# First tokens loaded in 4 KB rows, conditioning sums undivided and behind the 1/rms chain, tokens scaled block by block

## The chip, the cores and the metric

The kernel runs on one core of a Trainium2 chip. The metric is the device time of one execution in microseconds (us). TensorE (PE) multiplies matrices and transposes, VectorE (DVE) and ScalarE (ACT) work elementwise, GpSimd (POOL) does slower elementwise work, and SyncE (SP) issues the transfers from and to memory (DMA).

## The reference

A two-layer encoder over 1024 tokens of width 1024. Each layer normalises the tokens, scales and shifts them by a conditioning vector, mixes tokens and adds the result back under a gate:

```python
c_act = jax.nn.silu(c)
for layer in range(DEPTH):
    mod = c_act @ ada_w[layer] + ada_b[layer]
    shift, scale, gate = jnp.split(mod, 3, axis=-1)
    h = rms_norm(x, norm_w[layer]) * (1.0 + scale[:, None, :]) + shift[:, None, :]
    y = even_mixer(h, ...) if layer % 2 == 0 else odd_mixer(h, ...)
    x = x + gate[:, None, :] * y
return rms_norm(x, final_norm)
```

In layer 0 the mixer begins with `proj = h @ w_in`. Everything that the change touches at the start serves to make `h` for the first 512 tokens and to multiply it with the first columns of `w_in`.

## The kernel before

The tokens are held transposed: the model's width lies on the partitions, in eight blocks of 128 (`kc` 0 to 7), and 512 tokens (a half) lie in a row. `xT[half]` is four tiles of 128 x 1024, each with two blocks side by side; `chunk(t, kc)` is one block of 128 x 512. fp32 precision is kept by splitting each factor of a product into a high part (`h`, rounded by a cast) and a low part (`l`, the remainder), so that a product takes three matmuls (`mm3`: high x high, low x high, high x low).

The start goes as follows. The first half's tokens are loaded block by block (`xT_half(0)`), ACT squares each block (`sq`), DVE adds the squares up, and PE transposes the sums so that DVE can reduce them over the width (`ss`). POOL raises the result to the power -1/2 (`r`), PE spreads it over all partitions in PSUM (`rp0`, the 1/rms of each token), and DVE scales the eight blocks by it. This is the 1/rms chain, `rstd_rows`.

Meanwhile the conditioning values are made: for each block `kc` a scale and a shift per channel, each a sum over 1024 products of a loaded row of `ada_t` with `cb` (`ada_sum`, `ada_mods`; results in `mods`). One such sum is a DVE instruction that multiplies, adds up and leaves its total to a short read-out instruction. In the trace it is CUSTOM_DVE_ANT_0 with DVE_READ_ACCUMULATOR2_ANT; in the built order both are called ISA. Before the change a sum is taken in two pieces of 512, into a small tile `ada..`, and one addition makes `mods` of the pieces.

Then, block by block, ACT makes the high part of `h` from the scaled tokens (`hT00h`, with `mods` as scale and bias) and `h` itself (`xT`), DVE subtracts them to the low part (`hT00l`), and PE multiplies four token tiles with two groups of weight columns, 416 wide (`c1_part`, weights `w1.`) and 512 wide (`c3_part`, weights `w3.`): 24 matmuls for a block. The weights are split by ACT (high) and DVE (low), two blocks to a load (`wload`). Behind the eighth block come PE's transposes for the second half's squares and the columns of `w2`.

All instructions are recorded (`Recorder`) and a planner with assumed durations lays them out in time. They are then emitted in the order of its start times, each engine running its own queue in order:

```python
for o in sorted(self.ops, key=lambda o: (o.start, o.i)):
    fn, a, kw = o.call
    fn(*[real(v) for v in a], **{k: real(v) for k, v in kw.items()})
```

That is why nearly every row of the trace bears the line L483. An operation's `after` (set by `behind`) keeps the planner from placing it before another one's planned start. It adds no wait on the chip.

Of the kernel before, what the change touches and what calls it, by code (L numbers as in the profile page):

```python
# [14 lines left out]
ALU = mybir.AluOpType  # L15
# [8 lines left out]
KC = D // P  # L24
# [481 lines left out]
def encoder_kernel(ctx: ExitStack, tc: tile.TileContext, xt, ada_t, w_c1, w_c2, w_c3, w_g0, w_uq, w_ukv, w_out0, w_v1,  # L506
                   w_f1, w_out1, cols_d, rows_d, tabs_d, out, dump=None):
    if dump is None:
# [12 lines left out]
    mhalf = const.tile([P, 16], F32, name="mhalf")  # L521
    tc.nc.vector.memset(mhalf, -0.5)

    nc = rec = Recorder(tc.nc, tc, psum, {"u": U_BUFS, "ua": UA_BUFS, "sm": SM_BUFS}, window=WINDOW,
                        reserve=RESERVE)
# [11 lines left out]
    def SM(name):  # L537
        return rec.tile(smp, [P, 16], F32, name, "sm")
# [13 lines left out]
    def behind(ins, mark):  # L552
        ins.after = mark
        return ins
# [8 lines left out]
    def load(o, i, mark=None):  # L563
        return behind(nc.sync.dma_start(out=o, in_=i), mark)
# [24 lines left out]
    def transposes(outs, ins, last):  # L589
# [3 lines left out]
        for j in order:  # L593
            with issue_after(m_):
                t_ = nc.tensor.transpose(out=outs(j), in_=ins[j], identity=ident)
            if last is not None:
# [5 lines left out]
    mods = const.tile([P, 32], F32, name="mods")  # L602
# [5 lines left out]
                                   op0=ALU.add, op1=ALU.mult)  # L608
    cb = U("cb")
    for j in range(2):  # L610
        pt = PT(f"cb{j}")
        for k in range(4):
# [7 lines left out]
                                   op0=ALU.add, op1=ALU.mult)  # L620
    g0 = const.tile([P, 16], F32, name="g0")
    nc.gpsimd.tensor_scalar(g0, cols[:, C_BG:C_BG + 16], 0.5, 0.0, op0=ALU.mult, op1=ALU.add)
    gcol = const.tile([P, 16], F32, name="gcol")
# [10 lines left out]

    def ada_sum(o, src, scale, first, name, mark, parts):

        s = U(name)
        load(s, src, mark)  # L640
        n = 1024 // parts
        for q in range(parts):
            c = slice(q * n, (q + 1) * n)
            nc.vector.tensor_tensor_reduce(out=s[:, c], in0=s[:, c], in1=cb[:, c], scale=scale,
                                           scalar=0.0 if q else first, op0=ALU.mult, op1=ALU.add, accum_out=o[q])

    def ada_mods(l, kc, mark=None):

        t = SM(f"ada{l}{kc}")
        k = 8 * l + kc  # L650
        for j in range(2):
            o = [t[:, 2 * q + j:2 * q + j + 1] for q in range(2)]
            scale, first = (0.5, cols[:, C_BSH + k:C_BSH + k + 1]) if j else (nwh[:, k:k + 1], a0[:, k:k + 1])
            ada_sum(o, ada_t[l * 24 + 8 * (1 - j) + kc], scale, first, f"ada{l}{kc}{j}", mark, 2)
        nc.vector.tensor_tensor(out=mods[:, 2 * k:2 * k + 2], in0=t[:, 0:2], in1=t[:, 2:4], op=ALU.add)

    def ada_gate(l, b, mark=None):
        for t in range(4 * b, 4 * b + 4):
            k = 8 * l + t
            ada_sum([gcol[:, k:k + 1]], ada_t[l * 24 + 16 + t], 0.25, g0[:, k:k + 1], f"adag{l}{t}", mark, 1)  # L660

    def A_col(l, kc):
        return mods[:, 16 * l + 2 * kc:16 * l + 2 * kc + 1]
# [14 lines left out]
    def rstd_rows(accs, name):  # L678

        n = accs[0].shape[1]  # L680
        nt = n // P
        v = None
        for k, acc in enumerate(accs):
            pt = PA(f"st{name}")
            for j in range(nt):
                m_ = nc.tensor.transpose(out=pt[:, j * P:(j + 1) * P], in_=acc[:, j * P:(j + 1) * P], identity=ident)
            ss = SM("ss")
            nc.vector.tensor_reduce(out=ss[:, 0:nt], in_=pt[:, 0:n].rearrange("p (t c) -> p t c", t=nt), axis=AX.X,
                                    op=ALU.add)
            if k == 0:  # L690
                nc.vector.tensor_scalar(ss[:, 4:4 + nt], ss[:, 0:nt], 1.0 / D, EPS, op0=ALU.mult, op1=ALU.add)
            else:
                nc.vector.scalar_tensor_tensor(out=ss[:, 4:4 + nt], in0=ss[:, 0:nt], scalar=1.0 / D, in1=v, op0=ALU.mult,
                                               op1=ALU.add)
            v = ss[:, 4:4 + nt]
        if name == "x0" and WARM[1]:
            warm(WARM[1], m_)
        r = SM("r")
        nc.gpsimd.tensor_tensor(out=r[:, 0:nt], in0=v, in1=mhalf[:, 0:nt], op=ALU.pow)
        pr = PA(f"rb{name}")  # L700
        for j in range(nt):
            m_ = nc.tensor.transpose(out=pr[:, j * P:(j + 1) * P], in_=r[:, j:j + 1].broadcast_to([P, P]), identity=ident)
        if name == "x0" and WARM[2]:
            warm(WARM[2], m_)
        return pr[:, 0:n]

    def rows_copy(pr, name):
        rb = U(f"rb{name}")[:, 0:pr.proto().shape[1]]
        nc.scalar.copy(rb, pr)
        return rb  # L710
# [51 lines left out]


    xT = {}

    def chunk(t, kc):
        return t[kc // 2][:, (kc % 2) * 512:(kc % 2 + 1) * 512]

    def xT_half(half):
        xT[half] = [U(f"xT{half}{k2}") for k2 in range(4)]  # L770
        acc = U(f"sq{half}")
        if half == 0:
            for kc in range(KC):
                load(chunk(xT[0], kc), xt[0, kc // 2][:, (kc % 2) * 512:(kc % 2 + 1) * 512])
            a, b = acc[:, 0:512], acc[:, 512:1024]
            for kc in range(KC - 1):
                add_squares((a, b)[kc % 2], chunk(xT[0], kc), kc < 2, f"sq0{kc}", nc.vector)
            nc.vector.tensor_tensor(out=a, in0=a, in1=b, op=ALU.add)
            last = U("sq07")[:, 0:512]
            add_squares(last, chunk(xT[0], KC - 1), True, "", None)  # L780
            return rstd_rows([a, last], "x0")
        else:
            eng = nc.vector if SQ_ENG[0] == "dve" else nc.gpsimd
            for k2 in range(4):
                load(xT[half][k2], xt[half, k2])
                add_squares(acc, xT[half][k2], k2 == 0, f"sq{half}{k2}", eng)
            eng.tensor_tensor(out=acc[:, 0:512], in0=acc[:, 0:512], in1=acc[:, 512:1024], op=ALU.add)
        return rstd_rows([acc[:, 0:512]], f"x{half}")
# [3 lines left out]

    marks = {}
    VA = [U(f"VA{j}", F32R).rearrange("p (t g s d) -> p t g s d", t=4, g=2, s=2) for j in range(2)]
    karaw = U("karaw").rearrange("p (t c) -> p t c", t=8)
    ckvraw = U("ckvraw").rearrange("p (t c) -> p t c", t=8)
# [47 lines left out]
    E1, E3 = E_START  # L846
    rp0 = xT_half(0)
    for kc in range(KC):
        c = chunk(xT[0], kc)
        nc.vector.tensor_tensor(out=c, in0=c, in1=rp0, op=ALU.mult)  # L850
    for kc in range(KC):
        ada_mods(0, kc)
        if kc % 2 == 0:
            w1 += wload([w_c1[kc // 2]], 416, f"w1{kc // 2}", hi_eng=START_ENG[0], lo_eng=START_ENG[1])
            w3 += wload([w_c3[kc // 2]], 512, f"w3{kc // 2}", hi_eng=START_ENG[2], lo_eng=START_ENG[3])
        modulate(0, kc, chunk(xT[0], kc), None, hT0[0][kc], "normed")
        for i in range(E1):
            c1_part(i, w1[kc:], [kc])
        for i in range(E3):
            m_ = c3_part(i, w3[kc:], [kc])  # L860
# [5 lines left out]
    rb0 = rows_copy(xT_half(1), "x1")  # L866
# [45 lines left out]
    for g in range(2):  # L912
# [5 lines left out]
        r = rstd_of(ss[:, 0:8], HD, 8)  # L918
# [3 lines left out]
        for b in range(2):  # L922
            for s in range(2):
                nc.vector.tensor_tensor(out=t2[:, :, b * 32 + s * 16:b * 32 + s * 16 + 16],
                                        in0=kr_[:, :, b * 32 + (1 - s) * 16:b * 32 + (1 - s) * 16 + 16],
# [903 lines left out]
```

## Time and profile before

| | |
|---|---|
| median of 3 runs | 1215.26 us (1213.6 to 1216.71) |
| profiled execution, own time | 1213.96 us |
| its span in the trace | 1211.9 us |
| PE busy | 1170.2 us (97% of the span) |
| DVE busy | 933.9 us (77%) |
| ACT busy | 660.4 us (54%) |
| POOL busy | 560.3 us (46%) |

The span is the time from the first to the last instruction in the trace; the 2.06 us between it and the execution's own time lie around it. Busy time is an average over stages with different limits: where an engine is nearly always busy over the whole span, the stretches in which it isn't are to be looked for.

### The profile page before, as it was taken

What the parts mean: (1) busy time and instruction counts of PE and PEld (TensorE: products, weight loads), DVE (VectorE), ACT (ScalarE), POOL (GpSimd) and SP (SyncE); (2) the same over time, 40 slices, a digit from 0 to 9 for tenths busy, and PEclk for the clock granted to TensorE, in tenths of its full rate; (3) what the DMA queues carried; (4) which work ended last, traced back from release to release, by engine and by line L of the source; (5) the groups of instructions that cost most, each with busy time, mean ns of one, the idle gap of its engine ahead of it and who ended that gap; (6) DMA issues with size and microseconds to landing.
All of it is one profiled execution on the core that took longest, in us unless ns stands there. A gap on an engine that the chain in (4) does not pass through costs nothing.

```text
span 1211.9 us, 17927 instructions
## 1 busy us (share of the span) xinstructions
PE 1170.2 (97%) x6320; PEld 987.2 (81%) x6320; DVE 933.9 (77%) x1787; ACT 660.4 (54%) x1348; POOL 560.3 (46%) x551
## 2 busy tenths in 40 slices
PE   6999899999999999999999999899999999999996
PEld 5898778787878778778778888788888888888896
DVE  7976497888687988888789996839876598788343
ACT  4643356666555777787768122227765456653212
POOL 0057764435465555444448233504465265367321
PEclk9999899999999999999999999899999999999999
DMA  9601123131122220101034663100111121045112
GB/s 352 253 1 58 56 83 122 35 105 34 61 68 79 79 70 19 36 1 52 2 143 167 240 250 143 67 18 1 36 53 53 52 88 53 19 166 199 70 71 70
DMA packets 37338, 106.72 MB, mean 88 GB/s; under 512 B 3840, under 2 KB 9472, under 8 KB 37248
## 3 DMA queue, kind: packets, MB, share of 16 engines
q1 hardware_dynamic: 36480, 103.48, 23.7%
q0 software_dynamic: 768, 2.10, 0.7%
q8 instruction: 49, 0.80, 0.3%
q14 instruction: 41, 0.34, 0.1%
HBM read 82.36 MB, written 23.20 MB: 87 GB/s over the span
## 4 chain that ended last, share of the span: by engine, by line
PE 83%; DVE 10%; ACT 3%; issue 1%; DMA 1%; POOL 0%; SPq 0%; POOLq 0%; DVEq 0%; ACTq 0%
PE psum L483 83%; DVE nm L483 2%; DVE hla L483 1%; DVE p L483 1%; DVE hT11l L483 1%; DVE xr L483 1%; ACT q L483 1%; DVE Qa L483 1%; DMA xT<-in_xt 1%; ACT Pa L483 0%; DVE q L483 0%; ACT p L483 0%; DVE hl L483 0%; DVE hlb L483 0%; DVE ada L483 0%
## 5 line engine op out<-in xcount | busy, mean ns | idle before, releaser
L483 DVE TENSOR_REDUCE nm<-psum 128x1 f32<-128x1024 f32 x128 | 155.3, 1217 | 18.9 <-PE psum L483 17.2
L483 POOL TENSOR_SCALAR p<-p,dn 128x384 f32<-128x384 f32 (+1 forms) x128 | 74.1, 596 | 159.1 <-DVE dn L483 79.2
L483 DVE TENSOR_TENSOR hla<-psum,hla 128x512 fp32r<-128x512 f32 x128 | 84.9, 681 | 25.0 <-ACT hla L483 24.5
L483 PE MATMUL psum<-hla,VA 128*128 128x512 f32 x256 | 94.4, 421 | 5.4 <-DVE hla L483 4.0
L483 ACT CAST hla<-psum 128x512 fp32r<-128x512 f32 x128 | 72.5, 593 | 43.5 <-PE psum L483 37.2
L483 PE MATMUL psum<-ident,Pa 128*128 128x128 f32 x512 | 93.8, 272 | 0.8 <-DVE q L483 0.8
L483 POOL TENSOR_SCALAR Pb<-Pb,rs 128x1024 f32<-128x1024 f32 x64 | 71.8, 1124 | 45.6 <-DVE rs L483 43.9
L483 PE MATMUL psum<-hlb,VB 128*128 128x512 f32 x256 | 90.8, 427 | 2.2 <-DVE hlb L483 1.5
L483 POOL TENSOR_SCALAR Pa<-Pa,rs 128x1024 f32<-128x1024 f32 x64 | 76.4, 1198 | 34.8 <-DVE rs L483 32.1
L483 ACT ACTIVATE Pa<-psum,nm 128x1024 f32<-128x1024 f32 x64 | 71.6, 1120 | 32.0 <-DVE nm L483 24.7
L483 DVE TENSOR_TENSOR hlb<-psum,hlb 128x512 fp32r<-128x512 f32 x128 | 82.2, 683 | 7.7 <-ACT hlb L483 6.9
L483 ACT ACTIVATE Pb<-psum,nm 128x1024 f32<-128x1024 f32 x64 | 71.8, 1123 | 25.1 <-DVE nm L483 22.2
L483 PE MATMUL psum<-k,q 128*128 128x512 f32 x256 | 84.0, 399 | 0.2 <-ACT Pb L483 0.2
L483 PE MATMUL psum<-ident,Pb 128*128 128x128 f32 x512 | 79.4, 272 | 0.0
L483 DVE CUSTOM_DVE_ANT_0 p<-psum,bias,rows_g 128x384 f32<-128x384 f32 (+1 forms) x128 | 70.2, 577 | 10.7 <-PE psum L483 9.7
L483 ACT ACTIVATE p<-p,nm 128x384 f32<-128x384 f32 (+1 forms) x128 | 74.0, 585 | 7.1 <-DVE nm L483 7.1
L483 PEld LDWEIGHTS psum<-ident,Pa 128*128 128x128 f32 x512 | 65.0, 140 | 12.5 <-DVE q L483 1.0
L483 ACT CAST hlb<-psum 128x512 fp32r<-128x512 f32 x128 | 68.9, 603 | 9.1 <-PE psum L483 7.8
L483 ACT COPY ot<-psum 64x512 f32<-64x512 f32 x64 | 37.4, 584 | 65.7 <-PE psum L483 65.0
L483 PEld LDWEIGHTS psum<-ident,Pb 128*128 128x128 f32 x512 | 63.2, 140 | 11.2
L483 POOL TENSOR_TENSOR sq<-sq,sq 128x256 f32<-128x256 f32 (+2 forms) x22 | 26.9, 1222 | 79.9 <-ACT sq L483 79.7
L483 PE MATMUL psum<-oTl,wo1h 128*128 128x256 f32 (+1 forms) x192 | 61.1, 319 | 0.0
(749 smaller groups left out, 3672.3 us busy)
## 6 DMA issues: line engine op xcount, KB each, us to landing
ada<-in_ada_t SPq DMA_DIRECT2D x32, 512.0 KB, 8.2
adag<-in_ada_t SPq DMA_DIRECT2D x16, 512.0 KB, 4.8
o<-spill SPq DMA_DIRECT2D x12, 512.0 KB, 6.5
wo0s<-in_w_out SPq DMA_DIRECT2D x8, 512.0 KB, 8.4
xr<-in_xt SPq DMA_DIRECT2D x8, 512.0 KB, 9.6
x_sp<-xr SPq DMA_DIRECT2D x8, 512.0 KB, 3.0
wo1s<-in_w_out SPq DMA_DIRECT2D x8, 512.0 KB, 5.8
x1r<-x_sp SPq DMA_DIRECT2D x8, 512.0 KB, 5.3
```

Of the source, the lines that this page charges most:

```text
L483: fn(*[real(v) for v in a], **{k: real(v) for k, v in kw.items()})
```

## The change

The first half's tokens are loaded as four transfers of 128 rows of 4 KB instead of eight of 128 rows of 2 KB. Each conditioning sum is one instruction over 1024 products that writes straight into `mods`. For layer 0 these sums may not be planned before the POOL power of the 1/rms chain (`late=marks["rstd", "x0"]`). The eight scalings of the tokens no longer stand together: each stands in its block's turn, and only the first reads 1/rms from PSUM. For the other seven ACT copies it into SBUF (`rb0`). The sums of layer 1 are undivided too; the gates' sums (`ada_gate`) were so already.

```diff
-    def ada_sum(o, src, scale, first, name, mark, parts):
+    def ada_sum(o, src, scale, first, name, mark, late=None):
 
         s = U(name)
         load(s, src, mark)
-        n = 1024 // parts
-        for q in range(parts):
-            c = slice(q * n, (q + 1) * n)
-            nc.vector.tensor_tensor_reduce(out=s[:, c], in0=s[:, c], in1=cb[:, c], scale=scale,
-                                           scalar=0.0 if q else first, op0=ALU.mult, op1=ALU.add, accum_out=o[q])
-
-    def ada_mods(l, kc, mark=None):
-
-        t = SM(f"ada{l}{kc}")
+        behind(nc.vector.tensor_tensor_reduce(out=s, in0=s, in1=cb, scale=scale, scalar=first, op0=ALU.mult,
+                                              op1=ALU.add, accum_out=o), late)
+
+    def ada_mods(l, kc, mark=None, late=None):
+
         k = 8 * l + kc
         for j in range(2):
-            o = [t[:, 2 * q + j:2 * q + j + 1] for q in range(2)]
             scale, first = (0.5, cols[:, C_BSH + k:C_BSH + k + 1]) if j else (nwh[:, k:k + 1], a0[:, k:k + 1])
-            ada_sum(o, ada_t[l * 24 + 8 * (1 - j) + kc], scale, first, f"ada{l}{kc}{j}", mark, 2)
-        nc.vector.tensor_tensor(out=mods[:, 2 * k:2 * k + 2], in0=t[:, 0:2], in1=t[:, 2:4], op=ALU.add)
+            ada_sum(mods[:, 2 * k + j:2 * k + j + 1], ada_t[l * 24 + 8 * (1 - j) + kc], scale, first, f"ada{l}{kc}{j}",
+                    mark, late)
...
-        nc.gpsimd.tensor_tensor(out=r[:, 0:nt], in0=v, in1=mhalf[:, 0:nt], op=ALU.pow)
+        marks["rstd", name] = nc.gpsimd.tensor_tensor(out=r[:, 0:nt], in0=v, in1=mhalf[:, 0:nt], op=ALU.pow)
...
-            for kc in range(KC):
-                load(chunk(xT[0], kc), xt[0, kc // 2][:, (kc % 2) * 512:(kc % 2 + 1) * 512])
+            for k2 in range(4):
+                load(xT[0][k2], xt[0, k2])
...
     rp0 = xT_half(0)
     for kc in range(KC):
+        ada_mods(0, kc, late=marks["rstd", "x0"])
         c = chunk(xT[0], kc)
-        nc.vector.tensor_tensor(out=c, in0=c, in1=rp0, op=ALU.mult)
-    for kc in range(KC):
-        ada_mods(0, kc)
+        nc.vector.tensor_tensor(out=c, in0=c, in1=rb0 if kc else rp0, op=ALU.mult)
+        if kc == 0:
+            rb0 = rows_copy(rp0, "x0")
```

How the planner's order moves is seen on two engines. First DVE, before the change, from the end of the first block's sums on (`xT00` holds blocks 0 and 1, `w10l0` and `w30l0` are the weights' low parts of blocks 0 and 1, `ada010` and `ada011` the rows for block 1's scale and shift):

```order
L483 TENSOR_TENSOR mods_81<-ada00_129 128x2
L483 TENSOR_TENSOR w10l0_134<-w10s0_132,w10h0_133 128x832
L483 TENSOR_TENSOR xT00_115<-xT00_115,psum_72 128x512 x2
L483 TENSOR_TENSOR xT01_116<-xT01_116,psum_72 128x512 x2
L483 TENSOR_TENSOR xT02_117<-xT02_117,psum_72 128x512 x2
L483 TENSOR_TENSOR xT03_118<-xT03_118,psum_72 128x512 x2
L483 TENSOR_TENSOR w30l0_137<-w30s0_135,w30h0_136 128x1024
L483 TENSOR_TENSOR hT00l0_92<-xT00_115,hT00h0_88 128x512
L483 ISA ada010_139,ada01_138<-ada010_139,cb_83,a0_85,nwh_84 128x512
L483 ISA ada01_138 128x1
```

The same place on DVE in the changed kernel, from the last step ahead of POOL's power (`ss_127`) on:

```order
L483 SCALAR_TENSOR_TENSOR ss_127<-ss_127,ss_126 128x4
L483 ISA ada000_129,mods_81<-ada000_129,cb_83,a0_85,nwh_84 128x1024
...
L483 ISA ada001_130,mods_81<-ada001_130,cb_83,cols_80 128x1024
...
L483 TENSOR_TENSOR xT00_115<-xT00_115,psum_72 128x512
L483 TENSOR_TENSOR w10l0_134<-w10s0_132,w10h0_133 128x832
L483 TENSOR_TENSOR w30l0_137<-w30s0_135,w30h0_136 128x1024
L483 ISA ada010_138,mods_81<-ada010_138,cb_83,a0_85,nwh_84 128x1024
...
L483 TENSOR_TENSOR hT00l0_92<-xT00_115,hT00h0_88 128x512
L483 ISA ada011_139,mods_81<-ada011_139,cb_83,cols_80 128x1024
...
L483 TENSOR_TENSOR xT00_115<-xT00_115,rbx0_131 128x512
```

Here the short read-outs behind the sums are left out. The first block's sums have moved from inside the chain to behind it, and seven of the eight scalings have moved from ahead of `w30l0` to their blocks' turns.

ACT in the changed kernel, at the same place (`rbx0` is the copy of 1/rms, a new instruction; before, `hT00h0` follows `w30h0` at once):

```order
L483 ACTIVATE sq07_125<-xT03_118 128x512
L483 CAST w10h0_133<-w10s0_132 128x832
L483 CAST w30h0_136<-w30s0_135 128x1024
L483 COPY rbx0_131<-psum_72 128x512
L483 ACTIVATE hT00h0_88<-xT00_115,mods_81 128x512
L483 ACTIVATE xT00_115<-xT00_115,mods_81 128x512
```

The copy waits for the first scaling on DVE, which reads the same bank of PSUM, and stands ahead of the first high part.

## Rows read from the trace of the kernel before

**Rows 1.** The page: its first line, and the chain's shares by engine.
```profile
span 1211.9 us, 17927 instructions
...
PE 83%; DVE 10%; ACT 3%; issue 1%; DMA 1%; POOL 0%; SPq 0%; POOLq 0%; DVEq 0%; ACTq 0%
```

**Rows 2.** Stages: length, busy us of PE, PEld, DVE, ACT, POOL; PEclk, DMA share, GB/s.
```profile
0.00:30.00 30.00, 20.13 (x112) 17.66 (x113) 22.92 (x51) 13.59 (x18) 2.46 (x9) 0.93 0.94 351
30.00:66.00 36.00, 36.00 (x169) 32.34 (x169) 32.45 (x71) 23.19 (x42) 0.00 (x0) 0.96 0.56 216
...
600.00:740.00 140.00, 139.06 (x694) 114.16 (x693) 130.06 (x216) 70.93 (x124) 59.48 (x47) 1.00 0.49 185
```

**Rows 3.** PE's waits, 0 to 100 us: us in total, times, longest.
```profile
PE psum L483 <- ACT hT00h L483: 2.1, 1, 2.1
...
PE psum L483 <- DVE w30l L483: 0.6, 1, 0.6
PE psum L483 <- DVE xT L483: 0.6, 1, 0.6
```

**Rows 4.** The chain in order of time, 0 to 70 us: start, us, what.
```profile
4.49 6.41 DMA xT<-in_xt
...
10.92 0.64 ACT sq L483
...
15.30 0.66 DVE ada L483 x2
...
16.12 1.42 POOL r L483
...
18.88 4.27 DVE xT L483 x7
...
24.88 3.42 DVE ada L483 x10
```

**Rows 5.** PE's timeline: start us, us, engine, line, operation, out<-in, count, idle before.
```profile
20.07 0.44 PE L483 MATMUL psum<-w10h,hT00h 128*128 128x416 f32 x1
...
35.95 0.35 PE L483 MATMUL psum<-w11h,hT00h 128*128 128x416 f32 x1
...
40.91 0.35 PE L483 MATMUL psum<-w11h,hT00h 128*128 128x416 f32 x1
...
65.84 0.60 PE L483 MATMUL psum<-ident,sq 128*128 128x128 f32 x4
```

**Rows 6.** DMA throughput in 40 slices of 1.5 us, 0 to 60 us.
```profile
GB/s 0 139 279 279 284 315 410 421 417 407 415 407 412 405 409 410 388 405 409 413 404 415 406 413 403 410 415 404 415 407 403 175 25 0 186 292 14 0 0 0
```

**Rows 7.** DVE's timeline, 18 to 33 us.
```profile
18.27 4.87 DVE L483 TENSOR_TENSOR xT<-xT,psum 128x512 f32<-128x512 f32 x8 [0.49 <-PE psum L483]
...
24.80 0.80 DVE L483 CUSTOM_DVE_ANT_0 ada<-ada,cb,a 128x512 f32<-128x512 f32 x1
...
25.53 0.74 DVE L483 CUSTOM_DVE_ANT_0 ada<-ada,cb,nwh 128x512 f32<-128x512 f32 x1
...
27.49 0.80 DVE L483 CUSTOM_DVE_ANT_0 ada<-ada,cb,a 128x512 f32<-128x512 f32 x1
...
30.93 1.01 DVE L483 TENSOR_TENSOR w11l<-w11s,w11h 128x832 fp32r<-128x832 f32 x1
31.86 1.21 DVE L483 TENSOR_TENSOR w31l<-w31s,w31h 128x1024 fp32r<-128x1024 f32 x1
```

**Rows 8.** The gates' sums (tile adag): duration ns, min/median/max.
```profile
L483 DVE CUSTOM_DVE_ANT_0 adag<-adag,cb,g x16: 1247/1273/1910, 219.0 to 997.5; 128x1024 f32<-128x1024 f32 x16
```

**Rows 9.** ACT's timeline, three places.
```profile
19.00 0.81 ACT L483 ACTIVATE hT00h<-xT,mods 128x512 fp32r<-128x512 f32 x1 [2.13 <-DVE xT L483]
...
44.00 1.05 ACT L483 CAST w2h<-w2s 128x1024 fp32r<-128x1024 f32 x1 [0.23 <-DMA w2s<-in_w_c]
...
69.20 0.59 ACT L483 COPY rbx<-psum 128x512 f32<-128x512 f32 x1 [2.05 <-PE psum L483]
```

**Rows 10.** PE's waits, 60 to 200 us: the longest.
```profile
PE psum L483 <- DVE Qa L483: 2.8, 1, 2.8
```

More of the change, by code (lines that the diff above doesn't have):

```diff
@@ L659, in ada_gate @@
             k = 8 * l + t
-            ada_sum([gcol[:, k:k + 1]], ada_t[l * 24 + 16 + t], 0.25, g0[:, k:k + 1], f"adag{l}{t}", mark, 1)
+            ada_sum(gcol[:, k:k + 1], ada_t[l * 24 + 16 + t], 0.25, g0[:, k:k + 1], f"adag{l}{t}", mark)
     def A_col(l, kc):
@@ L764, in encoder_kernel @@
     xT = {}
+    marks = {}
     def chunk(t, kc):
@@ L790, in encoder_kernel @@
     hT0 = [alloc_hT(0, 0), alloc_hT(0, 1)]
-    marks = {}
     VA = [U(f"VA{j}", F32R).rearrange("p (t g s d) -> p t g s d", t=4, g=2, s=2) for j in range(2)]
```

## The prediction

> **What bounds the kernel now.** I read the page first. The chain that ended last is PE for 83% and DVE for 10% of the 1211.9 us span [rows 1], so whatever makes PE idle or slow counts directly, and whatever happens beside a busy PE counts for nothing. The stages show where PE isn't busy: in the first 30 us it is busy for 20.13, from 30 to 66 for all 36 [rows 2]. The change sits in exactly these two stretches. PE's waits there that follow the first real matmul are 2.1, 0.6 and 0.6 us [rows 3]: it waits for ACT's high part of block 1, and for DVE.
>
> The chain in order of time says why. It runs from the load of the tokens, whose last piece is issued at 4.49 and lands at 10.90, over the last square (ends 11.56), past pieces of sums on DVE that stand in the queue between the steps of the chain, to POOL's power (16.12 to 17.54). Then come the scalings on DVE, which stand together, and after them a run of sums from 24.88 to 28.30 [rows 4]. So for ten microseconds DVE decides: first all eight blocks are scaled, though PE can use one, and then two blocks' sums are made before block 1 can go on.
>
> PE's own need in this stage is known. A block's 24 matmuls take 40.91 - 35.95 = 4.96 us when nothing is waited for; eight blocks take 39.7. In fact PE's first matmul starts at 20.07 and the transposes behind the eighth block at 65.84, which is 45.8 us [rows 5]. Of these 6.1 us too many, 3.3 are the three waits. Most of the rest, up to 2.8, is slow matmuls: the granted clock is 0.96 on average from 30 to 66 us [rows 2], just after the 2.1 us wait, so a part of this stretch ran at 1.2 GHz, the lower level.
>
> **The change step by step.** *The load.* During the 2 KB transfers the throughput is 279 to 315 GB/s; in the slices behind them, with 4 KB rows, it is 388 to 421 [rows 6]. The first bytes move in the slice from 1.5 us, which is half full, so from about 2.3 us. 2.1 MB at 408 GB/s take 5.1 us: 7.4. To the landing I add 0.8 us and take 8.2 for the last 512 KB instead of 10.90; the bounds are 7.9 and 10.9 (no quicker at all, if the low rate is that of any load's start). I lean to the fast end because the low rate lasts as long as the 2 KB rows do. All later loads queue behind these and move ahead by up to the same 2.7 us.
>
> The Trainium skill speaks against this term. By "DMA: Bandwidth & Descriptors", section Specifications, rows of 512 bytes already reach line rate, so 4 KB would be no better than 2 KB, the load would end at 10.90 as before, and the sum would be that of the second rival below. The rows contradict it unless the slow rate belongs to the start.
>
> *The squares.* A piece now holds two blocks, so behind the last landing stand two squares of 0.64 us [rows 4] with their handovers instead of one: 8.2 + 1.35 = 9.55 instead of 11.56. Call the end of the squares E.
>
> *From E to the power.* Before, this takes 4.56 us (11.56 to 16.12), of which two pairs of half sums that DVE ran between its small steps are in the chain with 0.67 + 0.66 us [rows 4]; they go. The small steps then follow one another directly and show their full delay (+0.25, an estimate), and in the new order one more filler transpose stands ahead (+0.15; four take 0.60 [rows 5]): E + 3.65.
>
> *From the power to the first scaling.* Before, 18.27 - 16.12 = 2.15 us [rows 4, 7]. Now DVE makes block 0's two sums in that gap. A sum over 1024 with one pointer operand takes 1.27 us, its median in the gates' sums [rows 8], and holds the queue for about 1.20; a second pointer adds 0.06, as the half sums show (0.80 against 0.74 [rows 7]). Both end at E + 6.0, 0.2 later than 1/rms would allow. This is the change's one new wait, and everything of the stage is queued behind it.
>
> *To the first matmul.* First scaling 0.69, the copy of 1/rms on ACT 0.59 (as its sister `rbx` took), the high part 0.81 [rows 9], and 0.15 of handovers: PE starts at E + 8.25 = 17.8 instead of 20.07. The copy costs 0.6 us on the path, which buys the other seven scalings nothing: from PSUM they take 0.61 each (4.87 for eight), and a subtraction in SBUF, 832 wide, takes as much per element (1.01) [rows 7].
>
> *DVE through the stage.* Four half sums held DVE from 24.80 to 27.49, plus 0.07 for the addition: 2.76 per block [rows 7]. Two whole ones hold it for 2.46. From E + 6.0 DVE has 8 scalings and 8 low parts (0.61 each), 7 pairs of sums, 4 weight splits of 0.93 and 6 of 1.14 (1.01 and 1.21 less the overlap that the start times show; two are `w2`): 37.5 us, so the last low part is done at E + 43.5 = 53.1. PE, if it never waits, begins block 7 at 17.8 + 34.7 = 52.5 and wants that low part four matmuls later, at 53.3. Followed block by block in the new order, DVE is ready 0.1 to 0.3 us ahead of PE each time. So PE becomes the bound of the stage with DVE right behind it; what either loses shows.
>
> *ACT* casts weights in its queue between the high parts, each when its load has landed. Before, the second `w2` cast began at 44.00, a DMA wait [rows 9]. In the new order it stands ahead of block 5's high part, which PE wants at 42.6. With loads 2.7 us earlier that cast ends at 42.35 and the high part at 43.2, 0.6 late.
>
> *The sum.* Without waits the stage ends at 17.8 + 39.7 = 57.5 instead of 65.84: 8.3 us less, of which 2.3 from the earlier start and 6.1 from waits and slow clock that go. I give back 1.3: 0.6 for that cast, 0.7 for DVE being late here and there or for part of a slow stretch. That is 7.0, with bounds of 0.2 and 3.8 for what is given back. *Layer 1's sums* shorten DVE's work by some 3 us near 700 us. PE is busy for 139.06 of the 140 us there [rows 2], so I count nothing, at most 1.
>
> *Afterwards* everything hangs on PE's results: the second half's chain and the rotary work on POOL and DVE start from matmuls of this stage and move along. The planner's order differs in places up to about 230 us and again in layer 1's preparation; elsewhere it is the same. The largest wait of PE in the first of these is 2.8 us for `Qa` [rows 10]; I allow 1.5 either way for it.
>
> The profiled execution's own time of 1213.96 less 7.0 gives 1207.0. The median of the runs shown is 1.3 above that execution, so I predict **1208.3**.
>
> **Rivals.** *No quicker load.* If 4 KB rows bring nothing, E is 10.9 + 1.35 = 12.25 and PE starts at 20.5, later than before. The waits still go, but the weight casts hold PE up for about 1.1 us (the second `w2` cast then ends at 45.05, as now, and block 5's high part at 45.9, wanted at 45.3). End of stage 61.3: 4.5 less, 1210.8. For it: the first slices of any load could be slow. Against: the rate rises just when the rows lengthen.
>
> *The slow clock stays.* PE still idles through the power's 1.42 us [rows 4], just ahead of the stage. If the clock is then granted at 1.2 GHz for two stretches of it, each at about 1.5 us (half of the 2.8 that slow matmuls cost before), 3.0 come on top of the 1.3. 4.0 us less: 1211.3. Against: the stage now has no such wait inside.
>
> *Given back later.* PE arrives at the rotary stage 7 us earlier, and if POOL's or DVE's work there is what it waits for, its waits grow by as much: 1213 to 1215. For it: PE waits there already [rows 10]. Against: that work starts from this stage's matmuls and should move with them.
>
> *The whole sums are slow.* The slowest of the gates' sums took 1.91 us, 0.64 above the median [rows 8]. Were all 16 of this stage like that, DVE would need 10.2 us more, the last low part would come at 63.3 and the stage end at 67.5 (4.2 of block 7 follow): 1.7 later than before, 1216.9. It turns to a loss from about 1.8 us a sum. Against: POOL does nothing from 30 to 66 us [rows 2], while it works beside the gates' sums.
>
> **How the numbers follow.** The forecast gets 0.60 (its own range is 1206 to 1210), no quicker load 0.14, the slow clock 0.08, given back later 0.12, slow sums 0.06. A measurement of this kernel tells about 0.3% (3.6 us) from no change. Faster by more are the first two and most of the third: 0.80. Within 0.3%: given back, the rest of the third, and slow sums up to 1.9 us: 0.16. Slower, for sums or waits beyond that: 0.04. The range goes down to 1204.5 (no stall, the order's 1.5 and layer 1's 1 in its favour) and up to 1212.5, which takes in the second and third case and leaves out the rest.
>
> **What would show it.** Right: the last tokens land near 8.2 us; the power starts near 13.2; DVE's first scaling follows two sums; PE's first 416-wide matmul is near 17.8; no wait of PE over 1 us until the transposes behind block 7, which start near 58.8. From there on each stage lies about 7 us earlier. Wrong: landing near 10.9; PE's clock at 0.5 inside the stage; single sums longer than 1.3 us on DVE between 13 and 55 us; or waits for `Qa`, `kll` or `wg0h` between 120 and 135 us that have grown by what the start gained.

## The result and the profile after

| | before | changed |
|---|---|---|
| median | 1215.26 us (1210.91 to 1217.21, 9 runs) | 1207.87 us (1206.55 to 1211.76, 9 runs) |
| span of the profiled execution | 1211.9 us | 1206.1 us |

The ratio is 0.9946, with a 95% interval of 0.9933 to 0.9958: 6.6 us less (5.1 to 8.1). Predicted were 7.0 less, and a median of 1208.3. The ratios here and below leave out one execution as slow, of 2981 us, of the kernel with the sums not held back.

The page of the changed kernel, first line and chain by engine, answers to [rows 1]: PE's share of the chain is the same.

```profile
span 1206.1 us, 17857 instructions
...
PE 83%; DVE 9%; ACT 5%; issue 2%; DMA 1%; POOL 0%; SPq 0%; POOLq 0%; DVEq 0%; ACTq 0%
```

The two stretches at the start answer to [rows 2]. PE is busy for 4.2 us more in the first, and at full clock in the second.

```profile
0.00:30.00 30.00, 24.31 (x134) 22.41 (x135) 23.57 (x38) 16.26 (x23) 3.17 (x9) 0.94 0.94 370
30.00:66.00 36.00, 36.00 (x197) 33.05 (x196) 32.27 (x49) 22.67 (x43) 3.90 (x4) 1.00 0.52 201
```

PE's waits from 0 to 100 us. Against [rows 3] the waits for ACT's high part and for DVE are gone. What is left lies ahead of the first matmul.

```profile
PE psum L483 <- POOL r L483: 2.4, 1, 2.4
PE psum L483 <- ACT sq L483: 1.9, 1, 1.9
PE psum L483 <- POOL ident masks.py:199: 1.4, 1, 1.4
```

The chain from 0 to 70 us, against [rows 4], and PE's timeline at the start and the end of the stage, against [rows 5]:

```profile
2.59 6.84 DMA xT<-in_xt
...
9.45 1.16 ACT sq L483 x2
...
13.51 2.13 POOL r L483
...
15.69 54.36 PE psum L483 x300
```

```profile
16.17 3.60 PE L483 MATMUL psum<-ident 128*128 128x128 f32 x20
19.42 0.69 PE L483 MATMUL psum<-w10h,hT00h 128*128 128x416 f32 x1
...
59.89 0.28 PE L483 MATMUL psum<-w2h,hT00h 128*128 128x256 f32 x1
```

The scalings and sums of DVE are out of the chain. From POOL's power on it is PE for 54 us. The stage, from PE's first matmul to the first behind block 7, took 45.8 us (20.07 to 65.84) and takes 40.5 (19.42 to 59.89). It ends 5.95 us earlier, and that is where the gain is made. But it begins only 0.65 earlier, where 2.3 were predicted: the last tokens land at 9.43 (8.2 predicted), the power takes 2.13 us (1.42 predicted), and filler transposes stretched to 3.60 us stand ahead of the first matmul (granted clock 0.74 from 15.0 to 19.4 us).

PE's waits from 60 to 200 us show that nothing of it is given back there: the one for `Qa` is 2.8 us, as in [rows 10], and all that are listed there add up to 6.3 us, against 6.2 before. The longest two:

```profile
PE psum L483 <- DVE Qa L483: 2.8, 1, 2.8
PE psum L483 <- DVE hla L483: 1.2, 2, 1.1
```

### The profile page after: what moved, and what is told of

Same layout as the page of the kernel before. It is cut to its first block, busy times and chain, and to the rows that moved or that the text cites. A ratio compares the mean times of both kernels' runs of the same rounds, so it can differ in the third digit from the quotient of the medians.

```text
span 1206.1 us, 17857 instructions
## 1 busy us (share of the span) xinstructions
PE 1168.0 (97%) x6320; PEld 987.8 (82%) x6320; DVE 927.7 (77%) x1707; ACT 660.5 (55%) x1349; POOL 563.2 (47%) x551
## 4 chain that ended last, share of the span: by engine, by line
PE 83%; DVE 9%; ACT 5%; issue 2%; DMA 1%; POOL 0%; SPq 0%; POOLq 0%; DVEq 0%; ACTq 0%
PE psum L483 83%; DVE nm L483 2%; DVE hla L483 1%; DVE hT11l L483 1%; ACT Pa L483 1%; DVE xr L483 1%; DVE p L483 1%; ACT k L483 1%; DVE Qa L483 1%; ACT q L483 1%; DMA xT<-in_xt 1%; DVE q L483 0%; ACT p L483 0%; ACT hlb L483 0%; DVE hlb L483 0%
## 5 line engine op out<-in xcount | busy, mean ns | idle before, releaser
L483 POOL TENSOR_SCALAR Pb<-Pb,rs 128x1024 f32<-128x1024 f32 x64 | 71.8, 1124 | 45.6 <-DVE rs L483 43.8
```

## The experiments

My theory after the result: the gain is that DVE no longer makes PE wait inside the stage, for which the scalings must be spread and the sums must stand behind the power; the load gives about what its own landing gains. Rivals: the quicker load carries it (all later loads move ahead too), or the undivided sums do (less work for DVE). All kernels were timed against the one before on the same chip; "us" below is the ratio's distance from 1, times 1215. The stage's start and end are read from PE's timeline of one profiled execution of each.

| kernel | ratio (95% interval) | us | stage start | end |
|---|---|---|---|---|
| before | | | 20.07 | 65.84 |
| changed | 0.9946 (0.9933 to 0.9958) | -6.6 | 19.42 | 59.9 |
| load alone | 0.9998 (0.9985 to 1.001) | -0.2 | 21.07 | 63.5 |
| spread scalings alone | 0.9967 (0.9955 to 0.998) | -4.0 | 21.15 | 61.6 |
| undivided sums alone | 1.0014 (1.0001 to 1.0027) | +1.7 | 23.59 | 65.5 |
| changed, 2 KB rows | 0.9956 (0.9938 to 0.9973) | -5.3 | 19.71 | 60.4 |
| changed, half sums | 0.9954 (0.9939 to 0.9969) | -5.6 | 17.49 | 61.3 |
| changed, sums not held back | 0.9993 (0.998 to 1.0006) | -0.9 | 23.89 | 63.9 |
| changed, sums behind the scaling | 0.9955 (0.9938 to 0.9973) | -5.5 | 18.64 | 60.1 |
| changed, 8 fillers | 0.9939 (0.9923 to 0.9955) | -7.4 | 17.66 | 59.4 |
| 8 fillers, no copy | 0.9974 (0.9962 to 0.9985) | -3.2 | 17.50 | 62.8 |
| 8 fillers, low parts on GpSimd | 1.0005 (0.9993 to 1.0018) | +0.6 | 17.72 | 64.4 |
| 8 fillers, other modulation | 0.9994 (0.9983 to 1.0005) | -0.7 | 17.78 | 63.0 |
| changed, once more | 0.9954 (0.9942 to 0.9967) | -5.6 | 17.76 | 59.3 |

The starts have to be read with the clock. The 20 filler transposes that PE makes behind the spreading of 1/rms take 2.35 us at full clock. In five of these executions they took 3.6 to 4.3, at the lower clock, and the first matmul came late, since the first high part was ready before the fillers were through: by 1.0 us in the changed kernel, 2.0 with the load alone, 1.4 with the spread scalings alone, 1.4 with 2 KB rows and 1.8 with the sums not held back. Before the change it was 0.3, and in the other kernels less than 0.1.

### One part alone

**Load alone**, on the kernel before:

```diff
-            for kc in range(KC):
-                load(chunk(xT[0], kc), xt[0, kc // 2][:, (kc % 2) * 512:(kc % 2 + 1) * 512])
+            for k2 in range(4):
+                load(xT[0][k2], xt[0, k2])
```

> The kernel before with only the four 4 KB transfers. Theory (the gain is that DVE no longer makes PE wait inside the first stage; the load gives only its own 1.5 us): the last tokens land near 9.4, the scalings still stand together, PE still waits some 2 us for the high part of block 1, the stage from first matmul to the transposes behind block 7 stays near 45.8 us, and the time falls by 1.0 to 1.5 us. Rival (the quicker load carries the gain, since every later load moves ahead with it): down by 4 us or more, and the stage is shorter than 43 us.

No change that can be measured. The interval (-1.8 to +1.2 us) still holds the theory's 1.0 to 1.5 less; the rival's 4 us lie outside it. As to the stage the theory was wrong and the rival right: it took 42.4 us, not 45.8, with 1.1 us of wait for block 1's high part instead of 2. The scalings still stand together, but in this order DVE splits both first weights before them. PE begins 1.0 us later, though the first high part is ready 0.75 earlier than before (19.06 against 19.81), because the fillers hold it up (PE's timeline, then ACT's):

```profile
17.30 4.01 PE L483 MATMUL psum<-ident 128*128 128x128 f32 x20
```

```profile
18.25 0.81 ACT L483 ACTIVATE hT00h<-xT,mods 128x512 fp32r<-128x512 f32 x1 [3.48 <-DVE xT L483]
```

In the profiled execution the stage ended 2.4 us earlier, but the span was only 1.2 shorter, and the median doesn't show it; one execution doesn't settle that, and I leave it open.

**Spread scalings alone**, with the copy of 1/rms:

```diff
     for kc in range(KC):
-        c = chunk(xT[0], kc)
-        nc.vector.tensor_tensor(out=c, in0=c, in1=rp0, op=ALU.mult)
-    for kc in range(KC):
         ada_mods(0, kc)
+        c = chunk(xT[0], kc)
+        nc.vector.tensor_tensor(out=c, in0=c, in1=rb0 if kc else rp0, op=ALU.mult)
+        if kc == 0:
+            rb0 = rows_copy(rp0, "x0")
```

> The kernel before with only the scalings spread over their blocks, and the copy of 1/rms; sums still in halves and between the chain's steps, 2 KB rows. Theory: PE starts 0.6 later (the copy), but DVE reaches block 1 some 4.3 us earlier; the waits of 2.1, 0.6 and 0.6 go, the stage takes 40.5 to 42 us, time 3 to 4.5 us below before. Rival (load): within 1 us of before. Second rival (the undivided sums are what relieves DVE): some 2 us of waits stay, time at most 2 below before.

As the theory has it: PE has no wait inside the stage and ends it 4.3 us earlier, although the sums are in halves, between the chain's steps, and the rows of 2 KB. It starts 1.1 later than before (0.6 expected); the high part is ready at 19.72 (19.81 before), and the rest is the fillers. All of PE's waits from 17 us to the end of the stage:

```profile
PE psum L483 <- POOL r L483: 3.2, 1, 3.2
```

**Undivided sums alone**, planned behind the power:

```diff
-        ada_mods(0, kc)
+        ada_mods(0, kc, late=marks["rstd", "x0"])
...
-        for q in range(parts):
...
+        behind(nc.vector.tensor_tensor_reduce(out=s, in0=s, in1=cb, scale=scale, scalar=first, op0=ALU.mult,
+                                              op1=ALU.add, accum_out=o), late)
```

> The kernel before with only the undivided sums, planned behind the power; scalings together, 2 KB rows. In its order the eight scalings stand between block 0's two sums. Theory: the power starts about 1.4 earlier (near 14.7), but block 0's shift now waits for eight scalings, so PE starts near 23 instead of 20; the stage behind it is short of waits; in all within 1.5 us of before. Second rival (the undivided sums carry the gain): 4 us or more below before.

Slower, if by little. Its chain shows why: seven scalings and then block 0's second sum stand ahead of the first high part, and PE waits 4.8 us for that.

```profile
17.21 4.26 DVE xT L483 x7
21.48 1.20 DVE ada L483
```

Alone the three parts give -0.2, -4.0 and +1.7, and all at once -6.6: the undivided sums behind the power are worth something only when the scalings are spread.

### One part undone

**2 KB rows again** (the load's edit turned round):

> The changed kernel with the tokens again in eight transfers of 2 KB rows; the order of the engines is otherwise nearly the same. Theory: landing near 10.9, the stage starts 1.5 later but keeps its 40.5 us, time 1.0 to 1.5 above the changed kernel, so still 5 below the one before. Rival (load carries the gain): 4 us or more above the changed kernel. If the slow first slices belong to the start and not to the rows, landing stays near 9.4 and nothing changes.

1.3 us of the gain go; the intervals overlap, so the time doesn't tell. PE starts 0.3 us later than in the changed kernel, not 1.5: the squares end at 10.69, against 10.61. The throughput of the first slices of 1.5 us tells the two loads apart, first of this kernel, then of the changed one:

```profile
GB/s 0 168 283 250 329 347 427 413 409 418 399 418 404 412 407 399 410 402 410 409 415 401 410 407 417 396 410 410 407 418 389 127 9 101 359 20 0 0 5 0
```

```profile
GB/s 0 67 382 404 404 415 417 404 413 412 410 408 403 416 407 396 407 410 407 410 412 407 407 409 412 401 407 410 412 410 230 19 66 334 82 0 0 0 5 0
```

From 3 to 9 us it is 250 to 347 with rows of 2 KB and 382 to 415 with rows of 4 KB, in the same slices, so it is the transfers that were slow and not the start. The edit halves the rows and the transfers alike. That the short rows are the slow part is seen from the DMA engines, whose packets filled their time in both kernels (from 3 to 9 us: packets, MB, share of the 16 engines' time):

```profile
q1 hardware_dynamic: 992, 1.81, 98.4%
```

```profile
q1 hardware_dynamic: 651, 2.41, 100.8%
```

A gap between small transfers would have left the engines idle. By the Trainium skill ("DMA: Bandwidth & Descriptors", Specifications), rows of 512 bytes already reach line rate; the measurement differs, and decides. Over the profiles the last tokens land at 10.0 to 10.9 in the four kernels with 2 KB rows, and at 8.7 to 9.4 with 4 KB rows.

**Half sums again**, for layer 0, still behind the power:

```diff
-            ada_sum(mods[:, 2 * k + j:2 * k + j + 1], ada_t[l * 24 + 8 * (1 - j) + kc], scale, first, ...)
+                for q in range(2):
+                    c = slice(q * 512, (q + 1) * 512)
+                    behind(nc.vector.tensor_tensor_reduce(out=s[:, c], in0=s[:, c], in1=cb[:, c], scale=scale,
+                                                          scalar=0.0 if q else first, op0=ALU.mult, op1=ALU.add,
+                                                          accum_out=t[:, 2 * q + j:2 * q + j + 1]), late)
+            nc.vector.tensor_tensor(out=mods[:, 2 * k:2 * k + 2], in0=t[:, 0:2], in1=t[:, 2:4], op=ALU.add)
```

> The changed kernel with layer 0's sums in halves again (and the additions of the pieces), still behind the power. Theory: the power takes 1.4 to 1.8 us instead of 2.13, DVE has 0.3 us more per block, which turns into up to 2 us of PE's waits for DVE in the stage; time 0.5 to 2 above the changed kernel. Rival (DVE has room enough, the halves cost nothing): within 0.3 us. Rival (the undivided sums carry the gain): 3 us or more above.

The stage takes 43.8 us with 2.0 us of PE's waits in it (1.3 for high parts, 0.7 for a low part), so DVE is late, as expected; at the end of the run 1.0 us of this is seen, within the intervals. The undivided sums don't carry the gain.

**Sums not held back**:

```diff
-        ada_mods(0, kc, late=marks["rstd", "x0"])
+        ada_mods(0, kc, late=None)
```

> The changed kernel with nothing that keeps the sums behind the power. In its order DVE makes one whole sum and both low weight parts between the chain's small steps, and three sums between the last of them and the first scaling. Theory: the power starts some 3 us later (near 16.5) and the first matmul comes near 22; the work done ahead is no longer in the stage, so it ends 1 to 3 us later than in the changed kernel; time 1 to 3 above it. Rival (the place of the sums doesn't matter, since the same DVE work is done either way): within 0.5 us.

This one line takes away nearly all of the gain, far more than I expected. The stage is as short as in the changed kernel (40.0 us) and begins 4.5 us later. DVE's timeline shows what stands ahead of the chain's small steps (`ss`, 0.16 each) and between them:

```profile
10.12 1.34 DVE L483 CUSTOM_DVE_ANT_0 ada<-ada,cb,a 128x1024 f32<-128x1024 f32 x1
...
12.59 1.27 DVE L483 CUSTOM_DVE_ANT_0 ada<-ada,cb,cols 128x1024 f32<-128x1024 f32 x1
...
14.40 1.01 DVE L483 TENSOR_TENSOR w10l<-w10s,w10h 128x832 fp32r<-128x832 f32 x1
15.33 0.16 DVE L483 TENSOR_SCALAR ss<-ss 128x4 f32<-128x4 f32 x1
15.40 1.21 DVE L483 TENSOR_TENSOR w30l<-w30s,w30h 128x1024 fp32r<-128x1024 f32 x1
16.54 0.15 DVE L483 SCALAR_TENSOR_TENSOR ss<-ss 128x4 f32<-128x4 f32 x1
```

The squares end at 9.87, as in the changed kernel's second execution (9.92, below), and the last small step comes 4.0 us later than there. The two sums account for 2.1 of this and the two weight parts, which the planner now sets ahead of the small steps, for 1.8. PE then waits 6.1 us for the power, and its fillers run at the lower clock (granted clock 0.51 from 17 to 24 us):

```profile
19.80 4.33 PE L483 MATMUL psum<-ident 128*128 128x128 f32 x20
```

The high part is ready at 22.06, near the 22 that I expected, and PE starts at 23.89: the 1.8 us between are what I hadn't reckoned with. So the loss belongs to this order as a whole, not to the sums alone. With half sums between the steps, the spread scalings alone kept 4.0 us.

**Sums behind the first scaling**, to see the power alone:

```diff
-        ada_mods(0, kc, late=marks["rstd", "x0"])
         c = chunk(xT[0], kc)
-        nc.vector.tensor_tensor(out=c, in0=c, in1=rb0 if kc else rp0, op=ALU.mult)
+        sc = nc.vector.tensor_tensor(out=c, in0=c, in1=rb0 if kc else rp0, op=ALU.mult)
+        if kc == 0:
+            sc0 = sc
+        ada_mods(0, kc, late=sc0)
```

> The changed kernel with the sums planned behind the first scaling instead of behind the power's start, so that no sum runs on DVE while GpSimd takes the power (a weight's low part does). Theory (a whole sum beside it draws the power out from about 1.4 to 2.12 us): the power takes 1.4 us or less and the first scaling comes 0.7 earlier, but block 0's shift is now due 2.5 us after it, so the first matmul comes 0.5 to 1.5 later than 19.42; time 0 to 1.5 above the changed kernel. Rival (the power's length has nothing to do with the sums): it stays at 2.1, and the first matmul comes 2 us later.

The power takes 1.03 us. DVE stands idle when it begins: the weight's low part starts 0.47 us into it. DVE's and POOL's timelines, of the changed kernel and of the one with half sums, show what draws it out:

```profile
13.40 1.34 DVE L483 CUSTOM_DVE_ANT_0 ada<-ada,cb,a 128x1024 f32<-128x1024 f32 x1
...
13.51 2.12 POOL L483 TENSOR_TENSOR r<-ss,mhalf 128x4 f32<-128x4 f32 x1 [10.47 <-DVE ss L483]
```

```profile
12.72 0.81 DVE L483 CUSTOM_DVE_ANT_0 ada<-ada,cb,a 128x512 f32<-128x512 f32 x1
...
12.84 1.59 POOL L483 TENSOR_TENSOR r<-ss,mhalf 128x4 f32<-128x4 f32 x1 [9.93 <-DVE ss L483]
```

DVE starts a sum 0.1 us ahead of the power. It ends at 14.74 and 13.53; the power ends 0.89 and 0.90 after that. In the kernel before, the half sum running at 16.12 ended at 16.64, and the power 0.89 later. It needn't be a sum: with the load alone a weight's low part of 1.01 us was in flight, and the power took 1.74 and ended 0.90 behind it. So POOL waits for the one DVE instruction in flight, however long it is. The Trainium skill ("GPSIMD Engine Reference", Specifications) says that the two engines contend for SBUF where a DVE instruction has two inputs there; these rows agree.

The time of this kernel doesn't differ from the changed one's within the intervals: its stage begins at 18.64 and ends at 60.1. PE waits 1.9 us for the high part that needs block 0's shift. It starts earlier than 19.42 all the same, since the fillers take 2.35 us here; against the changed kernel's second execution (below), where they do so too, it starts 0.9 later.

### The start of PE and what paces the stage

**8 fillers** instead of 20:

```diff
-WARM = (32, 14, 20)
+WARM = (32, 14, 8)
```

> The changed kernel with 8 instead of 20 filler transposes behind the spreading of 1/rms; everything else in the same order. Theory (the fillers, which run at 1.2 GHz from 17.08 on, hold PE's first matmul up after the high part is ready at 18.40): the first matmul starts near 18.5 instead of 19.42 and the stage ends 0.5 to 1.0 earlier, near 59.0; time 0.5 to 1.0 below the changed kernel. Rival (PE then only reaches DVE's low parts sooner, or the idle time keeps the clock down longer): the start moves but the stage's end doesn't, waits for the low parts appear, time within 0.3 of the changed kernel or above it.

**The changed kernel once more**, with no edit:

> The changed kernel itself, on the same chip as the run before it: 1207 to 1209, and if its squares end near 9.9 instead of 10.61, as they did in five of six other runs with the 4 KB load, the first matmul still starts where the fillers end, about 0.6 earlier than 19.42.

These two belong together. The 17.66 of the 8 fillers can't be put down to them, since in the second execution of the very same program all 20 take 2.35 us instead of 3.60, and PE starts at 17.76, which is 1.66 us earlier and not the 0.6 expected:

```profile
15.48 2.35 PE L483 MATMUL psum<-ident 128*128 128x128 f32 x20
17.76 0.46 PE L483 MATMUL psum<-w10h,hT00h 128*128 128x416 f32 x1
...
59.31 0.28 PE L483 MATMUL psum<-w2h,hT00h 128*128 128x256 f32 x1
```

Its granted clock is 1.00 in both stretches, while the first execution was at 1.2 GHz for the fillers (0.94 on average from 0 to 30 us). Of the 1.66 us between the two starts, 0.7 come from the squares, which end at 9.92 instead of 10.61, and 1.0 from the fillers' clock. So in these two the fillers hold PE up only where the clock falls there. And it hardly matters: 1.66 us earlier at the start are 0.6 at the end, and nothing in the median; 8 fillers start as early and end as early. Neither can be told from the first timing of the changed kernel, so I name no better version. What stops PE is seen in ACT's timeline, of the second execution and then of the first:

```profile
42.43 1.05 ACT L483 CAST w2h<-w2s 128x1024 fp32r<-128x1024 f32 x1 [0.22 <-DMA w2s<-in_w_c]
43.39 0.81 ACT L483 ACTIVATE hT00h<-xT,mods 128x512 fp32r<-128x512 f32 x1
```

```profile
42.50 1.06 ACT L483 CAST w2h<-w2s 128x1024 fp32r<-128x1024 f32 x1 [0.23 <-DMA w2s<-in_w_c]
43.45 0.81 ACT L483 ACTIVATE hT00h<-xT,mods 128x512 fp32r<-128x512 f32 x1
```

The second `w2` cast waits for its load, and block 5's high part stands behind it. The cast begins at 42.4 to 42.8 in every variant of the changed kernel with 4 KB rows, whether PE started at 17.5 or at 23.9; with 2 KB rows, at 43.8 to 44.2. Block 5's high part is there at 44.2, and three blocks of 4.96 us follow: the stage can't end ahead of 59.1. An execution that starts at 19.42 reaches block 5 at 44.93 and just misses this bound.

**8 fillers and no copy** of 1/rms:

```diff
-        nc.vector.tensor_tensor(out=c, in0=c, in1=rb0 if kc else rp0, op=ALU.mult)
-        if kc == 0:
-            rb0 = rows_copy(rp0, "x0")
+        nc.vector.tensor_tensor(out=c, in0=c, in1=rp0, op=ALU.mult)
```

> The same with 8 fillers, and no copy of 1/rms: all eight scalings read PSUM. Theory (the copy stands on the path with 0.6 us and buys nothing): the first matmul near 17.9 and the stage's end 0.5 earlier than with 8 fillers alone; 1.0 to 1.5 below the changed kernel. Rival (DVE bounds the stage as soon as PE starts earlier): the end stays at that of 8 fillers, with PE waiting for DVE inside the stage.

Both views were wrong: 4.2 us slower than with the copy. DVE's last scaling and PE's timeline show it:

```profile
51.09 0.68 DVE L483 TENSOR_TENSOR xT<-xT,psum 128x512 f32<-128x512 f32 x1
```

```profile
52.35 0.39 PE L483 MATMUL psum<-w30h,hT00h 128*128 128x512 f32 x1
52.58 0.39 PE L483 MATMUL psum<-w30l,hT00h 128*128 128x512 f32 x1
```

The stage adds up eight accumulators, each in a PSUM bank. 1/rms left in PSUM keeps a bank until the eighth scaling at 51.09, and only after it does PE make the eighth accumulator's matmuls of blocks 0 to 6: 21 of 0.227 us, 4.8 us. Until then a block gives PE three matmuls less, and it waits 3.3 us for ACT's high parts, which wait for DVE's scalings and, in block 5 (1.95 us), for the `w2` cast. The copy buys the bank.

**8 fillers, three low parts of `w3` on GpSimd**:

```diff
-            w3 += wload([w_c3[kc // 2]], 512, f"w3{kc // 2}", hi_eng=START_ENG[2], lo_eng=START_ENG[3])
+            w3 += wload([w_c3[kc // 2]], 512, f"w3{kc // 2}", hi_eng=START_ENG[2], lo_eng="pool" if kc else START_ENG[3])
```

> The changed kernel with 8 fillers, and with the low parts of the second, third and fourth w3 tiles made by GpSimd, which does nothing in this stage, instead of VectorE. It takes 3 times 1.14 us off DVE's queue. Theory (with 8 fillers PE starts at 17.7, but DVE and ACT right behind it set the pace, so the stage ends only 0.5 earlier): with DVE relieved the stage ends near 58.0 to 58.5 instead of 59.4, and PE's waits inside it go; time about 1 below the changed kernel. Rival (ACT's casts, which follow the loads, set the pace, not DVE): the end stays at 59.4. Rival (GpSimd beside DVE makes DVE's sums longer than 1.34 us): the end moves back.

The theory falls: the gain is lost. ACT's timeline shows the larger part of it, then PE's:

```profile
28.58 0.89 ACT L483 CAST w12h<-w12s 128x832 fp32r<-128x832 f32 x1 [4.79 <-DMA w12s<-in_w_c]
```

```profile
31.67 0.45 PE L483 MATMUL psum<-w11h,hT00h 128*128 128x416 f32 x1 [3.34 <-ACT hT00h L483]
```

In the planner's new order the third `w1` cast and the third `w3` cast stand ahead of block 2's high part, and ACT waits 4.79 us for their load; with 8 fillers alone that high part is made at 25.74, ahead of them. Of the 5.1 us that PE waits in this stage, 4.75 are for high parts and 0.36 for a low part. Beside that, GpSimd slows DVE down. One of the three places, POOL's and DVE's timelines:

```profile
38.65 2.40 POOL L483 TENSOR_TENSOR w33l<-w33s,w33h 128x1024 fp32r<-128x1024 f32 x1 [5.28 <-ACT w33h L483]
```

```profile
39.32 2.27 DVE L483 TENSOR_TENSOR hT00l<-xT,hT00h 128x512 fp32r<-128x512 f32 x1 [1.13 <-ACT xT L483]
```

A subtraction of 0.69 us that starts while POOL works ends 0.54 us after POOL (41.59 against 41.05), so it took 1.58 too long; the other two places cost 0.65 and 0.73. The planner's order also moved these subtractions ahead of the next sums, where DVE idles for ACT (1.74, 2.06 and 1.13 us). How much of the loss would stay with the casts in their old place wasn't tried.

**8 fillers, other modulation** for blocks 1 to 7:

```diff
-        nc.vector.tensor_tensor(out=c, in0=c, in1=rb0 if kc else rp0, op=ALU.mult)
         if kc == 0:
+            nc.vector.tensor_tensor(out=c, in0=c, in1=rp0, op=ALU.mult)
             rb0 = rows_copy(rp0, "x0")
...
-        modulate(0, kc, chunk(xT[0], kc), None, hT0[0][kc], "normed")
+        modulate(0, kc, chunk(xT[0], kc), rb0, hT0[0][kc], "dve" if kc else "normed")
```

> The changed kernel with 8 fillers, and with blocks 1 to 7 modulated in another way: one DVE instruction multiplies the tokens by scale and 1/rms together, ACT makes only the high part, and one DVE instruction adds the shift and subtracts the high part. DVE keeps two instructions per block (0.06 us longer for a pointer each), ACT loses seven of 0.81 us and the low part no longer waits for ACT's second result. Theory (with 8 fillers the stage is paced by ACT's and DVE's queues right behind PE): waits on high and low parts shrink and the stage ends at 58.0 to 59.0 instead of 59.4; time 0.5 to 1.5 below the changed kernel run beside it. Rival (DVE's own work paces it): the end stays at 59.4 or comes 0.5 later, since DVE has 0.9 us more in all; time the same.

Also lost, and by neither view. ACT's timeline:

```profile
28.64 0.89 ACT L483 CAST w12h<-w12s 128x832 fp32r<-128x832 f32 x1 [5.67 <-DMA w12s<-in_w_c]
29.91 1.05 ACT L483 CAST w32h<-w32s 128x1024 fp32r<-128x1024 f32 x1 [0.39 <-DMA w32s<-in_w_c]
30.86 0.72 ACT L483 ACTIVATE hT00h<-xT,mods 128x512 fp32r<-128x512 f32 x1
```

With ACT freer the planner put two casts, which wait for their loads, ahead of a high part. ACT stands idle for 5.67 us, and PE then waits 3.4 us for that high part, as with the low parts on GpSimd. Such an order is the same bound as above, met earlier: a cast in ACT's queue holds up everything behind it until its load has landed.

## Why the prediction came out right, step by step

*The load.* Right in kind, the saving too large: the landing at 9.43 in the first execution and at 8.7 in the second (2.60 and 6.1), not at 8.2. The rate was as predicted, but the first bytes move later: 67 GB/s in the slice from 1.5 us against 139 in [rows 6]. The 0.8 us added for the landing stood on no row. A part that was overlooked takes more: with two blocks to a transfer ACT begins its squares near 4.9 instead of 4.05 and needs 5.0 us for the eight, so they end near 9.9 even where the last tokens land early. E was 10.61 and 9.92, predicted 9.55.

*From E to the power.* 2.90 us in both executions, predicted 3.65. Not two of the half sums but three stood in the chain: the one ahead of the first `ss` step held that step up as well.

*The power.* 2.13 us, taken as 1.42. This is the term that was missed: the sum queued behind the last small step starts first and is now twice as long. The two sums did not hold the first scaling up, as the prediction had it (by 0.2); they end at 15.94, and the scaling waits for PE until 16.38. The errors of these three terms cancel nearly: the first scaling came at E + 5.8, predicted E + 6.0.

*The first matmul.* 17.8 predicted, 19.42 in the first execution and 17.76 in the second; the difference is the clock on the fillers (1.0) and the end of the squares (0.7). That 17.76 lies so near 17.8 is luck: E was 0.4 later and the steps behind it 0.4 shorter. That the copy "buys the other seven scalings nothing" is right for their own length (0.69 us with a start every 0.60, as from PSUM), but not for the stage: without the copy it loses 3.4 us, for the bank. The price showed in [rows 3], in the wait of 0.6 us for `xT`, where PE stops until the eighth scaling is through (18.27 + 4.87):

```profile
23.20 0.49 PE L483 MATMUL psum<-w30h,hT00h 128*128 128x512 f32 x1 [0.57 <-DVE xT L483]
```

*The stage.* PE-bound, no wait in it over 1 us: right. No stretch at the lower clock: right but for the first three matmuls of the first execution, which start 0.49, 0.35 and 0.31 us apart instead of 0.19 and cost 0.6. Its end was predicted at 58.8 and came at 59.89 and 59.31. The give-back for the `w2` cast was the right mechanism, with the load's error in it: 0.6 was reckoned with loads 2.7 us earlier. They came 1.5 earlier (42.50 against 44.00 in [rows 9]), so the high part was ready at 44.2 and not at 43.2. A PE that came to block 5 at the predicted 42.6 would have waited 1.6; it came later, and waited 0.4 in the second execution and not at all in the first.

*Afterwards* the stages lie about 5.4 to 6.7 us earlier up to 750 us, and `Qa`'s wait is the same. "Given back later" fell. So did "slow sums": the undivided sums take 1.34 and 1.28 us in the stage. The 1.34 is over the 1.3 named as a sign of being wrong, but the prediction's own price for a sum with two pointers is 1.33. "No quicker load" is answered by the throughput. "The slow clock stays" came true only for the fillers and the three matmuls behind them.

The net, 6.6 against 7.0, is right partly because errors of opposite sign met. The median is nearer to its forecast (0.4) than the parts are, and that is luck: the stage ended 0.5 to 1.1 us later than predicted, and the 1.3 us added to get from the profiled execution to the median weren't there, as the profiled execution is the median. The measured parts say that spreading the scalings makes the larger share (-4.0 alone), and that with undivided sums the gain is kept only when they are held back (-0.9 without, in the order that the planner then makes).

## What to carry to other kernels

A long instruction that an engine may run at any time belongs behind the short steps of a chain in that engine's queue: one planner constraint that adds no work was worth 4.7 to 5.7 us here, by the sums and by what else the planner moved with them. When a stage has become PE-bound, look for the next bound before moving its start: here a cast behind a late load held the end at 59 us, and 1.7 us at the start bought 0.6. Look, too, at what a planner moves beside the edit: in two of the variants a cast that waits for its load came to stand ahead of a high part, and PE waited over 3 us for it. Ask of a copy out of PSUM what the bank is needed for, not only what the copy's reader saves.

## What was unexpected of the hardware

POOL's power of 128 x 4 takes 1.03 us when DVE is idle at its start, and otherwise ends 0.9 us after the DVE instruction that was in flight then: 1.41, 1.59 and 2.12 us for what was left of sums of 512 and 1024. The other way round, a DVE subtraction that begins during a POOL subtraction of 128 x 1024 ends 0.54 us after it, in all three places (1.34, 1.42 and 2.27 us instead of 0.69). One that begins 0.47 us into the power takes its usual 1.02.

The same program was granted the lower clock (1.2 GHz) on its fillers in one execution and not in another: 3.60 against 2.35 us for 20 transposes, after waits of PE for the power of 2.4 us in both.

Rows of 2 KB moved at 250 to 347 GB/s and rows of 4 KB at 382 to 415, in the same slices of two otherwise like kernels, with the DMA engines' time full in both.
